# Moving operand tiles in SBUF: a two-layer diffusion-transformer kernel with new places for its weight, retention and column tiles

## The chip, the core and the metric

The kernel runs on one core of a Trainium2 chip. The metric is the device time of one execution in microseconds (us), lower is better. The core's engines are named as in the profile: PE (TensorE matmul) and PEld (its weight loads), DVE (VectorE), ACT (ScalarE), POOL (GpSimd) and SP, whose queue issues most DMAs.

## The reference

The model has two layers over 256 latent tokens `x` and 256 context tokens `ctx`, width 1024. Each layer modulates its input with a shift and a scale taken from a conditioning vector, mixes tokens, adds the gated result to the residual, normalizes, and does the same with an MLP.

```python
for i in range(2):
    mod = silu(c) @ ada_w[i] + ada_b[i]                 # shift, scale, gate, twice (and for ctx)
    h, hc = x * (1 + sc1) + sh1, ctx * (1 + sc1c) + sh1c
    y, yc = retention(h, hc) if i == 0 else neighbourhood_attention(h, hc)
    x = layer_norm(ALPHA * x + g1 * y)
    h = x * (1 + sc2) + sh2
    x = layer_norm(ALPHA * x + g2 * (square(relu(h @ mlp_w1[i])) @ mlp_w2[i]))   # 1024 -> 4096 -> 1024
    # in layer 0 ctx takes the same two steps; in layer 1 it ends here
```

Retention has 4 heads. A head projects to q and k (256 columns each), v and a gate g (512 each), forms masked scores over the 512 tokens, normalizes `scores @ v` per token, multiplies by `silu(g)` and multiplies the result (512 columns) by its rows of `ret_w_o`. All is float32.

## The kernel before

A matrix product in float32 is made of three products of a shorter float type (float32r): each operand is held as a high part and the low rest, and `mm3` issues high x high, high x low, low x high into one PSUM bank. `nc.tensor.matmul` takes a stationary operand (`lhsT`, 128 columns, loaded by an LDWEIGHTS on PEld) and a moving operand (`rhs`, 256 or 512 columns here). While PE streams the moving operand of one matmul, PEld loads the stationary operand of the next.

Weights come in units of 512 KB, `[128, k, ncol]` with 1024 numbers to a partition. `specs` lists all units in the order of their use. `fetch` loads the next one (`raw`, issued by SP), ACT casts it to the high part `hi`, and `lows` lets DVE subtract to get the low part `lo`. `hi` and `lo` come from two pools, `hip` and `lop`, of five buffers each (`WB`), 4096 bytes to a partition. `take` hands out units and fetches ahead. In the first phase, which goes by chunks of 128 rows, the class `Weights` uses the same two pools with 768 columns.

What is stationary and what moves:

- First MLP (layer 0), first product (`mm1`, and `ctx_mm1` for the context half of the first two): the weight unit is stationary, `hTh`/`hTl` (the modulated input, `[128, 8, 512]`) moves. Sixteen steps in all: two halves `hf` of eight `fp`, each with two units. Steps 0 and 1 of the first half go in 256-wide matmuls (latent half, then context half), the other fourteen in 512-wide ones, 48 matmuls a step.
- First MLP, second product (`mm2`): `hid`, the squared relu of the first product, is stationary, the unit moves. Two `hf`, two column halves, eight units `u`, 24 matmuls of 512 columns a unit.
- Retention: q and k with the unit stationary, v and gate with the unit moving. The head's output, transposed by `to_oT` into `oh` (high, ACT) and `ol` (low, DVE), is stationary for `tok_mm`, which has the `ret_w_o` units moving: bank `pw`, 96 matmuls a head, 384 in all.
- Layer 1: the neighbourhood attention (banks `pn`, `pnv`, `pqk`, `ppt`, `pav`, `pnw`), then an MLP whose first product has 256-wide matmuls. Its input is kept 448 bytes further on in `hTh`/`hTl` (`AT = 7 * LINE`, `LINE` being 16 numbers), and its opening (`p1t`) has these tiles stationary.

Tiles are laid out in SBUF in the order of their pools: small ones (`smp`), columns and constants (`cpool`: among them `cT`, `misc`, `lgn`, then `R`, `hTh`, `hTl`), `raw`, the weights, eight scratch tiles (`scp`), and nine slots of 8 KB (`arena`, taken by `slot`) that hold `hid`, `oh`, `ol` and others in turn. In the built program before, `hTh` starts at byte 40,608 of a partition, the first `hi` at 97,952, the first `lo` at 118,432 and slot 0 at 155,296: all of the large tiles are 32 bytes past a multiple of 64, and all stand alike within 512 bytes. So the stationary and the moving operand of nearly every 512-wide matmul start at the same place of a 512-byte stretch.

The order of instructions on ACT, DVE, POOL and PE is a scheduler's, except where `InOrder` pins it (`act.on`, `pe.on` and so on); SP keeps program order. Every instruction is recorded by a helper, so the profile gives line 84 for nearly all; tiles tell them apart.

Of the kernel before, what the change touches and what calls it, by code (L numbers as in the profile page):

```python
# [10 lines left out]
F32 = mybir.dt.float32  # L11
F32R = mybir.dt.float32r
# [5 lines left out]
P = 128  # L18
D = 1024
KC = D // P  # L20
NT = 512
# [3 lines left out]
DK = 256  # L25
DV = 512
# [10 lines left out]
LINE = 16  # L37
# [67 lines left out]
def kernel(  # L105
# [23 lines left out]
    pe, act, dve, pool, sp = (  # L129
        InOrder(tc, getattr(nc, e), e in PIN)  # L130
        for e in ("tensor", "scalar", "vector", "gpsimd", "sync")
    )
    ec = ctx.enter_context

    WB = 5
    smp = ec(tc.tile_pool(name="smp", bufs=4))
    cpool = ec(tc.tile_pool(name="cpool", bufs=1))
    rawp = ec(tc.tile_pool(name="rawp", bufs=4))
    hip = ec(tc.tile_pool(name="hip", bufs=WB))
    lop = ec(tc.tile_pool(name="lop", bufs=WB))  # L140
    scp = ec(tc.tile_pool(name="scp", bufs=8))
    arena = ec(tc.tile_pool(name="arena", bufs=1))
    dram = ec(tc.tile_pool(name="dram", bufs=1, space=DRAM))
    psp = ec(tc.tile_pool(name="psp", bufs=8, space=PSUM))

    def small(pool_, n, tag, **kw):

# [4 lines left out]
    def nm(s):  # L152
        uid[0] += 1
        return f"{s}_{uid[0]}"
# [4 lines left out]
    def slot(i, shape, dt, s):  # L159

        return arena.tile(shape, dt, tag=f"s{i}", name=nm(s))
# [4 lines left out]
    def tsl(t):  # L166
        return slice(t * P, (t + 1) * P)
# [6 lines left out]
    def mm3(o, a, b, start, stop):  # L174
        (ah, al), (bh, bl) = a, b
        pe.matmul(o, lhsT=ah, rhs=bh, start=start, stop=False)
        pe.matmul(o, lhsT=ah, rhs=bl, start=False, stop=False)
        pe.matmul(o, lhsT=al, rhs=bh, start=False, stop=stop)
# [4 lines left out]
    specs = []  # L183

    def w_rows(wt, r0, nr, c0, ncol):
        specs.append((wt[r0 : r0 + nr, c0 : c0 + ncol], nr // P, ncol))
# [17 lines left out]
    def spec_w1(l, f0):  # L204
        for u in range(2):
            w_rows(mlp_w1[l], 512 * u, 512, f0, 256)

    for hf in range(2):
        for fp in range(8):
            spec_w1(0, hf * 2048 + fp * 256)  # L210
        for half in range(2):
            for u in range(8):
                w_rows(mlp_w2[0], hf * 2048 + u * 256, 256, half * 512, 512)

    NW, NWO = nat_w_in[0], nat_w_o[0]
# [35 lines left out]
    units = []  # L251
# [3 lines left out]
    def fetch(n, in_scratch=False, at=None):  # L255

        for src, k, ncol in specs[len(units) : len(units) + max(n, 0)]:
            raw = rawp.tile([P, k, ncol], F32, tag="raw", name=nm("raw"))
            sp.dma_start(out=raw[:], in_=src.rearrange("(k p) n -> p k n", p=P))
            if in_scratch or len(units) in scratch_units:  # L260
                hi, lo = Rows([scr("hi", F32R) for _ in range(k)]), Rows([scr("lo", F32R) for _ in range(k)])
                for i in range(k):
                    act.copy(out=hi[:, i, :], in_=raw[:, i, :])
                    pending.append((lo[:, i, :], raw[:, i, :], hi[:, i, :]))
                units.append((hi, lo))
                continue
            if at is None:
                hi = hip.tile([P, k, ncol], F32R, tag="hi", name=nm("hi"))
                lo = lop.tile([P, k, ncol], F32R, tag="lo", name=nm("lo"))
            else:  # L270
                both = slot(at, [P, 2, k, ncol], F32R, "hilo")
                hi, lo = both[:, 0], both[:, 1]
            act.copy(out=hi[:], in_=raw[:])
            pending.append((lo[:], raw[:], hi[:]))
            units.append((hi, lo))
# [33 lines left out]
    ident = cv("ident")  # L309

    lnT = cpool.tile([P, 2, 2, 2, KC], F32, tag="lnT", name="lnT")
    cT = cpool.tile([P, KC, 16, 2], F32, tag="cT", name="cT")
    scol = cpool.tile([P, 2, KC], F32, tag="scol", name="scol")
    bcol = cpool.tile([P, 2, KC], F32, tag="bcol", name="bcol")
    acol = cpool.tile([P, 3, 2, KC], F32, tag="acol", name="acol")
# [43 lines left out]
    still = scr("still", F32R)  # L359
    dve.memset(still[:, :256].bitcast(F32), 1.0)  # L360

    misc = cpool.tile([P, 40], F32, tag="misc", name="misc")
    mhalf, onecol, lgm = misc[:, 0:1], misc[:, 1:34], misc[:, 36:40]
    dve.memset(mhalf[:], -0.5)

# [139 lines left out]
    def bg_stream():  # L505


        plan = []
        for l, w, part in (
            list(EARLY)  # L510
            + [(1, 0, 0), (1, 0, 1), (1, 0, 2), (1, 1, 0), (1, 1, 1), (1, 1, 2)]
        ):
            sh, sc, g = 3 * w * D, (3 * w + 1) * D, (3 * w + 2) * D
            offs = (sh + 512 * part, sc + 512 * part) if part < 2 else (g, g + 512)
            for n in range(KC):
                plan.append((l, w, part, offs, n))
        nxt = bg_load(*plan[0])
        yield
        for step, (l, w, part, offs, n) in enumerate(plan):
            raw = nxt  # L520
            if step + 1 < len(plan):
                nxt = bg_load(*plan[step + 1])

            nt = 2 if l == 0 or (w == 0 and part < 2) else 1
            if n == 0:
                red = smp.tile([P, 2, 32], F32, tag="red", name=nm("red"), bufs=2)
            if (l, w, part) in EARLY:
                dve.on = True
                for kk in range(2):
                    for t in range(nt):  # L530
                        weigh(spare(t), raw[:, kk, :], t, 2 * (n % 4) + kk, n % 4 == 0 and kk == 0)
                dve.on = False
                if n % 4 == 3:
                    yield
                    for t in range(nt):
                        folded(red, spare(t), t, 512 * (n // 4), 512)
            else:
                if n == 0:
                    acc = slot(S_VL, [P, 2, D], F32, "acc")
                for t in range(nt):  # L540

                    dve.on = n == 0 and (w, part) == (0, 0)
                    weigh(acc[:, t], raw[:].rearrange("p a n -> p (a n)"), t, n, n == 0)
                    dve.on = False
                if n == KC - 1:
                    for t in range(nt):
                        folded(red, acc[:, t], t, 0, D)
            if n == KC - 1:
                if part < 2:
                    due.append(lambda a=(l, w, red, 4 * part, nt): ada_columns(*a))  # L550
                else:
                    due.append(lambda a=(l, w, red, nt): ada_gate(*a))
            yield
# [162 lines left out]
    S_TH, S_TL, S_VH, S_VL, S_GS, S_SH, S_SL, S_T0, S_T1 = range(9)  # L716
# [20 lines left out]
    class Weights:  # L737
# [9 lines left out]

        def high(self, cols=slice(0, DK + DV)):
            if cols.start == 0:
                self.hi = hip.tile([P, DK + DV], F32R, tag="hi", name=nm("hi"))  # L750
            act.copy(out=self.hi[:, cols], in_=self.raw[:, cols])

        def low(self, cols=slice(0, DK + DV)):
            if cols.start == 0:
                self.lo = lop.tile([P, DK + DV], F32R, tag="lo", name=nm("lo"))
            dve.tensor_sub(out=self.lo[:, cols], in0=self.raw[:, cols], in1=self.hi[:, cols].bitcast(F32))

    def chunk_loads(k):
# [49 lines left out]
    prs, pts, rows = {}, {}, {}  # L808
# [15 lines left out]

    def chunk_row(k, cols=slice(0, 2 * P)):
        if cols.start == 0:
            rows[k] = smp.tile([P, 256], F32, tag="row", name=nm("row"), bufs=1)
        dve.tensor_copy(out=rows[k][:, cols], in_=prs[k][:, cols])

    def chunk_columns(k):  # L830
# [46 lines left out]
    def part_v(k, a, b):  # L877
# [8 lines left out]
        out=lgn[:, 0], in_=ret_decay[0].rearrange("(o d) h -> o (d h)", o=1).broadcast_to([P, 8])  # L886
# [19 lines left out]
    w = ws[0]  # L906
# [98 lines left out]
    for h in range(RH):  # L1005
# [9 lines left out]
        else:  # L1015
# [15 lines left out]
            for u in range(4):  # L1031
                ((wh, wl),) = take(1)
                for t in range(4):
                    for kk in range(2):
                        k = 2 * u + kk
# [72 lines left out]
        for t in range(4):  # L1108
            po = bank("po")
            scs = list(range(4)) if t < 2 else [2, 3]  # L1110
            for i, sc in enumerate(scs):
                a, b = S[sc]
# [12 lines left out]
            if t == 0:  # L1125
                bg()

        oh = slot(S_TH, [P, 4, NT], F32R, "oh")
        ol = slot(S_TL, [P, 4, NT], F32R, "ol")

        def to_oT(t):
            pT = bank("pT")
            for i in range(4):
                pe.transpose(pT[:, tsl(i)], gs[:, t, tsl(i)], ident)
            pv_ = pT[:].rearrange("p (k t) -> p k t", k=4)
            act.copy(out=oh[:, :, tsl(t)], in_=pv_)
            pinned, dve.on = dve.on, True
            dve.tensor_sub(out=ol[:, :, tsl(t)], in0=pv_, in1=oh[:, :, tsl(t)].bitcast(F32))
            dve.on = pinned

        between = {4: lambda: to_oT(0), 5: lambda: to_oT(1)}
# [7 lines left out]
        def tok_mm(t, half, us):  # L1149
            pw = bank("pw")  # L1150
            for k in range(4):
                wh, wl = us[k // 2]
                mm3(pw[:], (oh[:, k, tsl(t)], ol[:, k, tsl(t)]), (wh[:, k % 2, :], wl[:, k % 2, :]), k == 0, k == 3)
            return pw

        def tok(t, half, us):
# [120 lines left out]
    for hf in range(2):  # L1277
# [65 lines left out]
        for half in range(2):  # L1343
# [66 lines left out]
            p = turn(0)  # L1410
# [9 lines left out]
            p = turn(1)  # L1420
# [423 lines left out]
    n = NS - 1  # L1844
# [369 lines left out]
```

## Time and profile before

| | |
|---|---|
| time, median of 3 runs | 1178.7 us (1178.62 to 1179.35) |
| span of the profiled execution | 1177.4 us |
| PE busy | 1167.3 us, 6821 matmuls |
| PEld busy | 985.6 us, 6821 loads |
| DVE / ACT / POOL busy | 844.6 / 480.6 / 212.5 us |
| DMA | 195.10 MB, mean 166 GB/s |

The time holds 1.3 us beside the span of the profiled execution. [...] What a matmul costs in a stream is the distance between two starts: the chain of waits gives it as the length of a merged piece over its count. In rows of groups, `p<-hi,hid` means that bank `p` is written from tiles `hi` and `hid`.

### The profile page before, as it was taken

What the parts mean: (1) busy time and instruction counts of PE and PEld (TensorE: products, weight loads), DVE (VectorE), ACT (ScalarE), POOL (GpSimd) and SP (SyncE); (2) the same over time, 40 slices, a digit from 0 to 9 for tenths busy, and PEclk for the clock granted to TensorE, in tenths of its full rate; (3) what the DMA queues carried; (4) which work ended last, traced back from release to release, by engine and by line L of the source; (5) the groups of instructions that cost most, each with busy time, mean ns of one, the idle gap of its engine ahead of it and who ended that gap; (6) DMA issues with size and microseconds to landing.
All of it is one profiled execution on the core that took longest, in us unless ns stands there. A gap on an engine that the chain in (4) does not pass through costs nothing.

```text
span 1177.4 us, 17745 instructions
## 1 busy us (share of the span) xinstructions
PE 1167.3 (99%) x6821; PEld 985.6 (84%) x6821; DVE 844.6 (72%) x1349; ACT 480.6 (41%) x819; POOL 212.5 (18%) x364
## 2 busy tenths in 40 slices
PE   9999999999999999999999999999999999999997
PEld 7788888888888889888888888889888878999886
DVE  3786678787888787757767675678577589877446
ACT  3643332222323246442212333137466666665341
POOL 0103001000200241780203000223343430000001
PEclk9999999999999999999999999999999999999999
DMA  9943544544355416757566665646344334766660
GB/s 276 276 130 104 161 143 140 152 147 152 118 169 175 141 60 214 189 112 217 171 190 197 212 199 190 201 141 204 83 135 139 111 115 155 222 209 197 233 212 36
DMA packets 140115, 195.10 MB, mean 166 GB/s; under 512 B 9936, under 2 KB 81136, under 8 KB 140032
## 3 DMA queue, kind: packets, MB, share of 16 engines
q1 hardware_dynamic: 131904, 182.03, 49.4%
q0 software_dynamic: 6976, 9.39, 3.9%
q10 hardware_dynamic: 1152, 2.56, 0.7%
q8 instruction: 53, 0.87, 0.3%
q14 instruction: 30, 0.25, 0.1%
HBM read 189.12 MB, written 5.75 MB: 166 GB/s over the span
## 4 chain that ended last, share of the span: by engine, by line
PE 94%; DMA 2%; SPq 1%; ACT 1%; DVE 1%; issue 0%; POOL 0%; ACTq 0%; DVEq 0%
PE p L84 44%; PE pw L84 7%; PE pg L84 7%; PE pq L84 7%; PE pv L84 7%; PE pn L84 5%; PE pnv L84 4%; PE po L84 3%; PE ppt L84 2%; PE pnw L84 1%; PE pS L84 1%; PE pav L84 1%; PE pqk L84 1%; SPq L84 1%; PE pt L84 1%; PE p1t L84 1%
## 5 line engine op out<-in xcount | busy, mean ns | idle before, releaser
L84 ACT CAST hi<-raw 128x1024 fp32r<-128x1024 f32 (+2 forms) x228 | 231.7, 1032 | 308.9 <-PE p L84 113.4
L84 DVE TENSOR_TENSOR lo<-raw,hi 128x1024 fp32r<-128x1024 f32 (+2 forms) x228 | 273.4, 1213 | 105.5 <-ACT hi L84 105.4
L84 PE MATMUL p<-hi,hid 128*128 128x512 f32 (+1 forms) x832 | 241.8, 373 | 0.0
L84 PEld LDWEIGHTS p<-hi,hid 128*128 128x128 f32 x832 | 152.1, 188 | 27.6
L84 PE MATMUL p<-hTh,lo 128*128 128x256 f32 (+1 forms) x512 | 165.8, 326 | 0.0
L84 PE MATMUL p<-hTl,hi 128*128 128x256 f32 (+1 forms) x512 | 165.8, 326 | 0.0
L84 PE MATMUL p<-hTh,hi 128*128 128x256 f32 (+1 forms) x512 | 162.9, 328 | 0.0
L84 PE MATMUL p<-lo,hid 128*128 128x512 f32 (+1 forms) x416 | 155.2, 373 | 0.0
L84 DVE SCALAR_TENSOR_TENSOR acc<-rawa,scol,acc 128x1024 f32<-128x1024 f32 x56 | 74.5, 1342 | 66.0 <-DMA rawa<-in_ada_w_dram 66.0
L84 PEld LDWEIGHTS p<-hTh,lo 128*128 128x128 f32 x512 | 96.4, 188 | 8.8
L84 PEld LDWEIGHTS p<-hTl,hi 128*128 128x128 f32 x512 | 96.4, 188 | 8.7
L84 PEld LDWEIGHTS p<-hTh,hi 128*128 128x128 f32 x512 | 94.2, 188 | 8.7
L84 PEld LDWEIGHTS p<-lo,hid 128*128 128x128 f32 x416 | 78.4, 188 | 13.7
L84 DVE SCALAR_TENSOR_TENSOR strips<-rawa,scol,strips 128x512 f32<-128x512 f32 x112 | 78.6, 762 | 0.0
L84 ACT CAST hid<-r 128x256 fp32r<-128x256 f32 (+1 forms) x64 | 31.9, 500 | 111.2 <-DVE r L84 111.2
L84 POOL TENSOR_TENSOR rstd<-rstd,misc 128x1 f32<-128x1 f32 x28 | 19.1, 684 | 212.4 <-DVE rstd L84 211.4
L84 POOL TENSOR_TENSOR R<-R,acc 128x512 f32<-128x512 f32 x16 | 25.8, 1633 | 168.8 <-DVE acc L84 168.8
L84 ACT ACTIVATE s<-s,mn 128x512 f32<-128x512 f32 x64 | 45.5, 713 | 22.0 <-DVE mn L84 22.0
L84 PE MATMUL pw<-hi,oh 128*128 128x512 f32 x128 | 51.0, 398 | 0.0
L84 PE MATMUL pg<-hi,hTh 128*128 128x512 f32 x128 | 50.6, 395 | 0.0
L84 PE MATMUL pq<-hTh,hi 128*128 128x512 f32 x128 | 49.3, 395 | 0.8 <-ACT hTh L84 0.5
L84 PE MATMUL pw<-hi,ol 128*128 128x512 f32 x128 | 49.9, 390 | 0.0
(238 smaller groups left out, 2278.5 us busy)
## 6 DMA issues: line engine op xcount, KB each, us to landing
raw<-in_mlp_w_dram SPq DMA_DIRECT2D x128, 512.0 KB, 4.2
rawa<-in_ada_w_dram SPq DMA_DIRECT2D x80, 512.0 KB, 3.9
raw<-in_ret_w_in_dram SPq DMA_DIRECT2D x42, 512.0 KB, 3.9
raw<-in_nat_w_in_dram SPq DMA_DIRECT2D x24, 512.0 KB, 4.3
rawq<-in_ada_w_dram SPq DMA_DIRECT2D x16, 512.0 KB, 6.2
raw<-in_ret_w_o_dram SPq DMA_DIRECT2D x16, 512.0 KB, 3.4
bias<-rpb_rows POOLq DMA_DIRECT2D x32, 128.0 KB, 2.9
raw<-in_nat_w_o_dram SPq DMA_DIRECT2D x8, 512.0 KB, 3.8
```

The source lines that it names most:

```text
L84: r = f(*args, **kwargs)
```

## The change

- `hip` and `lop` become one pool `wpp`. Its tile holds both parts of a unit, 2 x 1024 numbers and 128 to spare. `wpair(at)` gives the high part at `at` and the low part 4096 bytes behind it. `Weights` takes its two parts from the same pool, both when the high part is made.
- `places` gives a start to the units of the first MLP: step `fp` of the first product `64 * fp` bytes into its tile, unit `u` of the second product `64 * u`. All others start at 0.
- `oh` and `ol` change from `[128, 4, 512]` to `[128, 2, 512, 2]`: two row blocks of the head's output are interleaved, so that a stationary operand is read with a step of 8 bytes.
- `misc` grows from 40 to 112 numbers, which moves all behind it; `cT` and the two `row` buffers go to arena slots, `red` shares the buffers of `rt`. With all this `hTh` starts at byte 38,336, the first `w` at 95,680 and slot 0 at 155,584: the large tiles are at multiples of 64 bytes.

```diff
-    hip = ec(tc.tile_pool(name="hip", bufs=WB))
-    lop = ec(tc.tile_pool(name="lop", bufs=WB))
+    wpp = ec(tc.tile_pool(name="wpp", bufs=WB))
...
+    WSLOT = 1024
+    WPAD = 128
+
+    def wpair(at):
+
+        both = wpp.tile([P, 2 * WSLOT + WPAD], F32R, tag="w", name=nm("w"))
+        return both[:, at : at + WSLOT], both[:, at + WSLOT : at + 2 * WSLOT]
...
+    places = {}
     for hf in range(2):
         for fp in range(8):
+            for u in range(2):
+                places[len(specs) + u] = LINE * fp
             spec_w1(0, hf * 2048 + fp * 256)
         for half in range(2):
             for u in range(8):
+                places[len(specs)] = LINE * u
                 w_rows(mlp_w2[0], hf * 2048 + u * 256, 256, half * 512, 512)
...
             if at is None:
-                hi = hip.tile([P, k, ncol], F32R, tag="hi", name=nm("hi"))
-                lo = lop.tile([P, k, ncol], F32R, tag="lo", name=nm("lo"))
+                hi, lo = (w.rearrange("p (k n) -> p k n", k=k) for w in wpair(places.get(len(units), 0)))
...
-    cT = cpool.tile([P, KC, 16, 2], F32, tag="cT", name="cT")
+    cT = arena.tile([P, KC, 16, 2], F32, tag="s1", name="cT")
+    row2 = arena.tile([P, 2, 256], F32, tag="s0", name="row2")
...
-    misc = cpool.tile([P, 40], F32, tag="misc", name="misc")
+    misc = cpool.tile([P, 40 + 72], F32, tag="misc", name="misc")
...
-                red = smp.tile([P, 2, 32], F32, tag="red", name=nm("red"), bufs=2)
+                red = smp.tile([P, 2, 32], F32, tag="rt", name=nm("red"), bufs=2)
...
             if cols.start == 0:
-                self.hi = hip.tile([P, DK + DV], F32R, tag="hi", name=nm("hi"))
+                self.hi, self.lo = (w[:, : DK + DV] for w in wpair(0))
...
-            rows[k] = smp.tile([P, 256], F32, tag="row", name=nm("row"), bufs=1)
+            rows[k] = row2[:, k % 2]
...
-        oh = slot(S_TH, [P, 4, NT], F32R, "oh")
-        ol = slot(S_TL, [P, 4, NT], F32R, "ol")
+        oh = slot(S_TH, [P, 2, NT, 2], F32R, "oh")
+        ol = slot(S_TL, [P, 2, NT, 2], F32R, "ol")
...
-            act.copy(out=oh[:, :, tsl(t)], in_=pv_)
+            oh_, ol_ = (o[:, :, tsl(t)].rearrange("p a t i -> p a i t") for o in (oh, ol))
+            act.copy(out=oh_, in_=pv_)
...
-                mm3(pw[:], (oh[:, k, tsl(t)], ol[:, k, tsl(t)]), (wh[:, k % 2, :], wl[:, k % 2, :]), k == 0, k == 3)
+                a, b = (o[:, k // 2, tsl(t), k % 2] for o in (oh, ol))
+                mm3(pw[:], (a, b), (wh[:, k % 2, :], wl[:, k % 2, :]), k == 0, k == 3)
```

PE's instructions, those of SP and those of POOL keep their order. The scheduler moves some on DVE and ACT, since both parts of a unit are now taken from their pool at the same point. Two places show the kind of move. On DVE, in retention head 1, between the rotation of the q projection's first half (`t_217`, later `t_185`) and its second (`t_218`, later `t_186`), `lo` and its `raw` being a weight unit for the same head. Before:

```order
L84 TENSOR_TENSOR qkl_1321<-t_217_1390,qkh_1320 128x256 [waits Activation_49]
L84 TENSOR_TENSOR lo_1419<-raw_1416,hi_1418 128x1024 [waits DMAHW3_49,PE_49,Activation_49]
L84 TENSOR_TENSOR t_218_1399<-pq_1323,cst_82 128x256 [waits Activation_49]
L84 TENSOR_TENSOR t_218_1399<-pq_1323,cst_82 64x256 x2
L84 TENSOR_TENSOR qkl_1321<-pq_1323,qkh_1320 128x256
L84 TENSOR_TENSOR t_218_1399<-t_218_1399 128x256 [waits DVE_49]
L84 TENSOR_TENSOR qkl_1321<-t_218_1399,qkh_1320 128x256 [waits Activation_49]
```

Now:

```order
L84 TENSOR_TENSOR qkl_1290<-t_185_1356,qkh_1289 128x256 [waits Activation_49]
L84 TENSOR_TENSOR t_186_1365<-pq_1292,cst_79 128x256 [waits Activation_49]
L84 TENSOR_TENSOR t_186_1365<-pq_1292,cst_79 64x256 x2
L84 TENSOR_TENSOR qkl_1290<-pq_1292,qkh_1289 128x256
L84 TENSOR_TENSOR t_186_1365<-t_186_1365 128x256 [waits DVE_49]
L84 TENSOR_TENSOR w_1384<-raw_1382,w_1384 128x1024 [waits DMAHW3_49,Activation_49]
L84 TENSOR_TENSOR qkl_1290<-t_186_1365,qkh_1289 128x256 [waits Activation_49]
```

The unit's subtraction stands four rows later, behind most of the second half's rotation, and has lost its wait for PE. On ACT, in the first half of the first MLP, around the casts of the two units of a step (`hi`, later `w`) and the relu of the step before (`r`). Before:

```order
L84 CAST hi_4453<-raw_4451 128x1024
L84 CAST hi_4459<-raw_4457 128x1024
L84 ACTIVATE r_4417<-p_684_4351 128x512
L84 CAST hid_4349<-r_4417 128x512
L84 ACTIVATE r_4511<-p_694_4449 128x512
```

Now:

```order
L84 CAST w_4364<-raw_4362 128x1024
L84 ACTIVATE r_4328<-p_599_4264 128x512
L84 CAST w_4369<-raw_4367 128x1024
L84 CAST hid_4262<-r_4328 128x512
L84 ACTIVATE r_4420<-p_607_4360 128x512
```

The relu of the second bank of a step now stands between the two casts.

More of the change, by code (lines that the diff above doesn't have):

```diff
@@ L749, in high @@
             if cols.start == 0:
-                self.hi = hip.tile([P, DK + DV], F32R, tag="hi", name=nm("hi"))
+                self.hi, self.lo = (w[:, : DK + DV] for w in wpair(0))
             act.copy(out=self.hi[:, cols], in_=self.raw[:, cols])
         def low(self, cols=slice(0, DK + DV)):
-            if cols.start == 0:
-                self.lo = lop.tile([P, DK + DV], F32R, tag="lo", name=nm("lo"))
             dve.tensor_sub(out=self.lo[:, cols], in0=self.raw[:, cols], in1=self.hi[:, cols].bitcast(F32))
@@ L1134, in to_oT @@
                 pe.transpose(pT[:, tsl(i)], gs[:, t, tsl(i)], ident)
-            pv_ = pT[:].rearrange("p (k t) -> p k t", k=4)
-            act.copy(out=oh[:, :, tsl(t)], in_=pv_)
+            pv_ = pT[:].rearrange("p (a i t) -> p a i t", a=2, i=2)
+            oh_, ol_ = (o[:, :, tsl(t)].rearrange("p a t i -> p a i t") for o in (oh, ol))
+            act.copy(out=oh_, in_=pv_)
             pinned, dve.on = dve.on, True
-            dve.tensor_sub(out=ol[:, :, tsl(t)], in0=pv_, in1=oh[:, :, tsl(t)].bitcast(F32))
+            dve.tensor_sub(out=ol_, in0=pv_, in1=oh_.bitcast(F32))
             dve.on = pinned
```

## The prediction

> **What bounds the kernel now.** I read the engines' busy times first, then PE's own waits, then the chain of waits in short windows.
>
> ```profile
> span 1177.4 us, 17745 instructions
> PE 1167.3 (99%) x6821; PEld 985.6 (84%) x6821; DVE 844.6 (72%) x1349; ACT 480.6 (41%) x819; POOL 212.5 (18%) x364
> ...
> PE 94%; DMA 2%; SPq 1%; ACT 1%; DVE 1%; issue 0%; POOL 0%; ACTq 0%; DVEq 0%
> ```
>
> ```profile
> PE pq L84 <- DVE still L84: 1.2, 1, 1.2
> PE pq L84 <- ACT hTh L84: 0.5, 1, 0.5
> PE pq L84 <- DVE hTh L84: 0.4, 1, 0.4
> ```
>
> PE is busy for 1167.3 of 1177.4 us, 94% of the chain that sets the end is PE, and its whole list of waits for other engines adds up to 2.1 us, all of it in bank `pq`. So nothing that ACT, DVE or the queues do sooner can pay. PE keeps its instructions and their order. What can move the time is what one matmul costs in a stream, so I worked that out from the chain of waits: start, length, bank, count. The length over the count is the distance between two starts.
>
> ```profile
> 464.98 105.17 PE p L84 x464
> 448.93 12.12 PE p L84 x101
> 803.97 12.15 PE pn L84 x100
> 1010.91 69.13 PE p L84 x610
> 996.06 8.03 PE p1t L84 x68
> ```
>
> 1. First MLP, 512 columns, both operands alike within 512 bytes: 105.17 / 464 = 226.66 ns.
> 2. First MLP, 256 columns, alike: 12.12 / 101 = 120.0 ns. `pn` in layer 1, 256 columns, alike: 121.5 ns with some interruptions in it.
> 3. Last MLP, 256 columns, where `AT` puts the moving operand 448 bytes on, so that the next stationary stands 64 bytes ahead of it within 512: 69.13 / 610 = 113.33 ns.
> 4. Its opening `p1t`, 256 columns, where the stationary tile is the one moved: it stands 64 bytes behind: 8.03 / 68 = 118.1 ns.
>
> Rows 1 and 2 differ by 106.66 ns for 256 columns. So 256 columns take 106.7 ns to stream, 512 take 213.3, and what is left is 13.3 ns at either width. It does not grow with the columns; it belongs to the handover from one matmul to the next. Row 3 has 6.7 ns of it, half as much, and row 4 11.4 ns. The three full values are 13.3, 6.7 and 113.3, all multiples of 6.67 ns: I call that a step. A 512-wide stream in this kernel pays two steps a matmul, and the only known way to pay one is another place of one operand against the other.
>
> [...]
>
> **The change part by part.**
>
> *Places in the first MLP.* First product: seven of eight steps get a place, 14 of 16 steps over both halves; one of them, step 1 of the first half, is 256 wide. 13 steps x 48 = 624 matmuls of 512 columns have the stationary 64 to 448 bytes ahead of the moving operand. Second product: 2 halves x 2 column halves x 7 units x 24 = 672, with the moving operand ahead. Together 1,296, some 190 for each of the seven distances. The 256-wide step has 96 matmuls at 64 bytes ahead, which is row 3: 96 x 6.67 = 0.6 us saved.
>
> For the 1,296 there is no row at 512 columns. Two of the seven distances have a 256-wide row: 64 ahead saves 120.0 - 113.3 = 6.7 ns, 64 behind saves 120.0 - 118.1 = 1.9 ns. Since what is left over is the same at both widths where both can be seen, I carry it over, and take the mean of the two for all seven: 4.3 ns x 1,296 = 5.6 us. The bounds on this side: 1.9 ns each is 2.5 us, 6.7 ns each is 8.6 us. On the far side a stream may fall out of step, as these rows of the timeline show (start, duration), after an interruption by other matmuls:
>
> ```profile
> 626.12 0.39 PE L84 MATMUL p<-hTl,hi 128*128 128x512 f32 x1
> 626.35 0.40 PE L84 MATMUL p<-hTh,lo 128*128 128x512 f32 x1
> 626.58 0.39 PE L84 MATMUL p<-hTh,hi 128*128 128x512 f32 x1
> 626.81 0.40 PE L84 MATMUL p<-hTl,hi 128*128 128x512 f32 x1
> 627.04 0.39 PE L84 MATMUL p<-hTh,lo 128*128 128x512 f32 x1
> ```
>
> They start 230 to 231 ns apart, some 4 ns over row 1, before the stream falls back to 226.7. Row 4 against row 3 is the same: 118.1 against 113.3. So the bound above zero is about 4.4 ns x 1,296 = 5.7 us lost.
>
> *Pairs in retention.* `tok_mm` has 384 matmuls of 512 columns whose stationary is now read with a step of 8 bytes; its start stays alike with the moving operand, or 4 bytes off. No row has a stationary with such a step.
>
> ```profile
> 214.96 16.12 PE pw L84 x71
> L84 ACT CAST oh<-pT x16: 580/587/592, 102.4 to 418.8; 128x512 fp32r<-128x512 f32 x16
> L84 DVE TENSOR_TENSOR ol<-pT,oh x16: 669/684/692, 105.3 to 419.7; 128x512 fp32r<-128x512 f32 x16
> L84 PE MATMUL pw<-hi,oh x128: 389/389/501, 106.8 to 436.4; 128*128 128x512 f32 x128
> ```
>
> Now it is 16.12 / 71 = 227.0 ns. The load passes the places of the moving operand at another pace, which may free a step (384 x 6.67 = 2.6 us) or cost the 4.4 ns of a stream out of step (1.7 us). I take half of the 4.3 ns above, as the start is unchanged: 0.8 us saved.
>
> The writers now write with a step of 8 bytes: 16 casts of 587 ns, 16 subtractions of 684 ns. Between no cost and twice as long, 16 x 1.27 = 20 us if nothing covered it. It is covered: the first subtraction starts at 105.3 and would end at 106.7 if doubled, while the first `pw` matmul starts at 106.8 and reads `oh` alone; later ones have a whole block of twelve `pw` matmuls (2.7 us) in between. I take zero.
>
> [...]
>
> *Multiples of 64 bytes.* Every 256- and 512-wide matmul reads rows that started 32 bytes past a multiple and no longer do. No row of before is aligned, so it has no price from one; bounds are zero and one step for each matmul (a rival, below). I take zero.
>
> *Shared tiles and moved subtractions.* A unit's parts come free together, so a cast waits also for the last reader of the low part, one or a few matmuls on (0.23 us each):
>
> ```profile
> ACT hi L84 <- PE p L84: 113.4, 49, 4.4
> DVE lo L84 <- ACT hi L84: 105.4, 87, 3.9
> ```
>
> ACT waits there already, 113.4 us in 49 times, and PE for none of these casts: there are five buffers, and a unit feeds 24 matmuls or 5.4 us. Behind a waiting cast on ACT stand a relu and the next cast; PE would see them first as a wait for `hi`, which it has nowhere. DVE is 72% busy. If this cover went, 0.2 us for each of some 100 units is 20 us; I see nothing that takes it away, so zero. `cT`, `row` and `red` are small and early: zero, with a few tenths either way.
>
> Sum: 5.6 + 0.6 + 0.8 = 7.0 us saved. The span becomes 1170.4; with the 1.3 us that the time holds beside it, 1171.7. The profiled execution stands at the median (1178.7), so nothing is added for that.
>
> **The rivals.**
>
> *A step falls everywhere, by alignment.* 256 columns are 1,024 bytes, and 106.7 ns are 16 steps: a step is as long as 64 bytes of the moving row. A row 32 bytes off touches one stretch of 64 more, at 512 columns as at 256, and that could be the step that row 3 still pays. Aligned, all would lose it: some 3,860 matmuls of 512 columns x 6.67 = 25.8 us gives 1153; the 256-wide ones too, some 890 at 120.0 by a step (5.9 us) and 671 of the last MLP by what the loads leave, as these 128-wide ones come no closer than 1.20 / 11 = 109 ns:
>
> ```profile
> 850.83 1.20 PE ppt L84 x11
> ```
>
> 671 x 4.3 = 2.9 us; in all 34.6 us, 1144. For it: both widths have the same remainder. Against it: the remainder may be the handover itself, and rows 2 and 3 are both 32 off.
>
> *Nothing but the 96.* A 512-wide matmul has 213 ns for a load that 256-wide ones fit into 113, so its two steps may not come from a meeting of the two reads at all. Then places do nothing: 1178.7 - 0.6 = 1178. For it: no 512-wide stream shows less than 226.66. Against it: all of them stand alike.
>
> *Slower: streams out of step.* Place: the first MLP from 462 to 792 us and the `pw` banks. The two steps of a 512-wide matmul stay, and a distance that is neither zero nor 64 ahead keeps streams from falling back into step, as 64 behind does in row 4. Price 4.4 ns each: (1,296 + 384) x 4.4 = 7.4 us, less 0.6: 1185.5. It decides from some 680 of the 1,680 on, since 680 x 4.4 - 600 ns is 2.4 us. For it: row 4 stays 4.8 ns above row 3 in the mean of its 68. Against it: even row 4 is below row 2.
>
> **How the numbers follow.** Forecast .46, 1171.7, its own range 1166.5 (all 1,296 and the 384 and the 96 a step lower, 11.8 us) to 1175.5 (all as row 4, 3.1 us). Alignment .18, 1144 to 1153, some of it with the places' gain on top. Nothing .14, 1178. Out of step .22, 1179 to 1185.5. About 0.2%, 2.4 us, is what a measurement of this kernel can tell from no change. Faster: all of alignment and nearly all of the forecast, .62. Same: the third case and what of the others ends there, .15. Slower: .23. The range of 8 in 10 leaves out the lower part of alignment and the last of the slow case: 1147 to 1184.
>
> **What would show it.** In the chain of waits of the changed kernel, the first MLP by its steps: 48 matmuls of 512 columns, 226.7 ns at step 0 and 220.0 at step 1 of the second half, 224 to 225 at step 7, between them in the others; in the second product, unit 1 like step 7 and unit 7 like step 1. `pw` near 225 in place of 227.0. `pq`, `pv`, `pg` unchanged at 226.7, and the last MLP at 113.3: if these fall to 220 and 109, alignment is right. Distances of 231 in the first MLP would show the slow rival, and a wait of PE for `w` that the cover has gone. The forecast is wrong if places other than 64 ahead save nothing.

## The result and the profile after

The changed kernel takes 1185.5 us (1185.41 to 1186.2), before 1178.7: a ratio of 1.0057, 95% interval 1.0037 to 1.0077. It is slower by 6.8 us, where 7.0 us faster was forecast. The range ended at 1184.

The head of the page of the changed kernel and PE's list of waits:

```profile
span 1183.5 us, 17741 instructions
PE 1173.8 (99%) x6821; PEld 988.9 (84%) x6821; DVE 845.0 (71%) x1349; ACT 483.2 (41%) x819; POOL 212.7 (18%) x364
...
PE 97%; DMA 1%; DVE 1%; ACT 1%; issue 0%; POOL 0%; ACTq 0%; DVEq 0%
```

```profile
PE pq L84 <- DVE still L84: 1.2, 1, 1.2
PE pq L84 <- DVE hTh L84: 0.4, 1, 0.4
PE pc L84 <- DMA brow<-in_ada_b_dram: 0.2, 1, 0.2
```

The span grew by 6.1 us and PE's busy time by 6.5, with the same 6,821 matmuls. Its waits are 1.8 us, none for `w`, `oh` or `ol`. So the loss is in what one matmul costs. The chain of waits of the changed kernel gives that for each step of the first MLP (start, length, bank, count). These are steps 0 to 7 of the first product's second half:

```profile
618.38 10.22 PE p L84 x45
630.37 9.80 PE p L84 x42
640.87 10.22 PE p L84 x44
651.79 10.31 PE p L84 x45
664.33 9.30 PE p L84 x41
674.31 10.50 PE p L84 x45
685.28 10.69 PE p L84 x46
698.43 8.70 PE p L84 x38
```

| next stationary ahead by, bytes | 0 | 64 | 128 | 192 | 256 | 320 | 384 | 448 |
|---|---|---|---|---|---|---|---|---|
| ns from start to start | 227.1 | 233.3 | 232.3 | 229.1 | 226.8 | 233.3 | 232.4 | 228.9 |

The table repeats every 256 bytes, and the first half's 512-wide steps, 128 to 448 ahead, give the same: 232.2, 228.9, 226.7, 233.3, 232.7 and 228.9 ns. 226.7 is the least, at 0 and 256; 64 ahead costs a whole step of 6.67 ns more. From the second product (unit 1, which is 64 behind or 448 ahead, and unit 7, 64 ahead), and from 256-wide streams 64 ahead (step 1 of the first half; the last MLP's first 48; the rest of it):

```profile
535.07 4.82 PE p L84 x21
568.09 5.14 PE p L84 x22
457.48 4.95 PE p L84 x42
1010.60 5.30 PE p L84 x45
1016.69 70.39 PE p L84 x621
```

The second product, where it is the weight that moves, follows the same table: 229.5 and 233.6. So in these rows it is the distance that counts, not which of the two operands was moved. The 256-wide streams give 117.9, 117.8 and 113.35 ns, all at the same distance. `pw`, whose stationary has the 8-byte step, and `pq`, which was not touched, with the load groups of `pw` in the changed kernel:

```profile
214.74 16.34 PE pw L84 x70
231.77 21.09 PE pq L84 x93
L84 PEld LDWEIGHTS pw<-w,oh 128*128 128x128 f32 x256 | 49.1, 196 | 8.9
```

`pw` went from 227.0 to 233.4 ns, and its loads take 196 ns, where those of `pq`, `pv`, `pg` and the MLPs have 188. `pq` stays at 226.8.

The sum from these rows, each against 226.7: 336 matmuls at 64 and 320 bytes x 6.6, 384 at 128 and 384 x 5.6, 384 at 192 and 448 x 2.3, 192 at 256 x 0.1: 2.2 + 2.2 + 0.9 + 0 = 5.3 us. `pw` adds 384 x 6.4 = 2.5, the 96 256-wide ones take away 96 x 2.1 = 0.2. That is 7.6 us, against 6.1 in the span and 6.8 in the time. The difference was not traced further; times of one kernel spread by more (the kernel before, 29 times on one chip: 1178.3 to 1182.0).

### The profile page after: what moved, and what is told of

It is laid out like the page before. It is cut to its first block, busy times and chain, and to the rows that moved or that the text cites. A ratio compares the mean times of both kernels' runs of the same rounds, so it can differ in the third digit from the quotient of the medians.

```text
span 1183.5 us, 17741 instructions
## 1 busy us (share of the span) xinstructions
PE 1173.8 (99%) x6821; PEld 988.9 (84%) x6821; DVE 845.0 (71%) x1349; ACT 483.2 (41%) x819; POOL 212.7 (18%) x364
## 4 chain that ended last, share of the span: by engine, by line
PE 97%; DMA 1%; DVE 1%; ACT 1%; issue 0%; POOL 0%; ACTq 0%; DVEq 0%
PE p L84 44%; PE pw L84 8%; PE pq L84 8%; PE pv L84 7%; PE pg L84 7%; PE pn L84 5%; PE pnv L84 4%; PE po L84 3%; PE ppt L84 2%; PE pnw L84 1%; PE pS L84 1%; PE pav L84 1%; PE pada L84 1%; PE pqk L84 1%; PE pt L84 1%; PE p1t L84 1%
## 5 line engine op out<-in xcount | busy, mean ns | idle before, releaser
L84 ACT CAST w<-raw 128x1024 fp32r<-128x1024 f32 (+2 forms) x224 | 231.0, 1038 | 324.1 <-PE p L84 164.9
L84 DVE TENSOR_TENSOR w<-raw,w 128x1024 fp32r<-128x1024 f32 (+2 forms) x224 | 272.2, 1223 | 111.4 <-ACT w L84 111.0
L84 PE MATMUL p<-w,hid 128*128 128x512 f32 (+1 forms) x1236 | 265.3, 375 | 0.0
L84 PEld LDWEIGHTS p<-w,hid 128*128 128x128 f32 x1236 | 218.8, 188 | 44.0
L84 PE MATMUL p<-hTh,w 128*128 128x256 f32 (+1 forms) x1024 | 240.8, 329 | 0.0
L84 PEld LDWEIGHTS p<-hTh,w 128*128 128x128 f32 x1024 | 171.9, 188 | 18.9
L84 PE MATMUL p<-hTl,w 128*128 128x256 f32 (+1 forms) x512 | 166.7, 328 | 0.0
L84 PEld LDWEIGHTS p<-hTl,w 128*128 128x128 f32 x512 | 96.3, 188 | 9.5
L84 PE MATMUL pw<-w,oh 128*128 128x512 f32 x256 | 81.7, 400 | 0.0
L84 PE MATMUL pq<-hTh,w 128*128 128x512 f32 x256 | 80.1, 392 | 0.4 <-DVE hTh L84 0.4
```

The lines of the kernel that those rows point to most:

```text
L84: r = f(*args, **kwargs)
```

## Experiments

All start from the changed kernel. The theory: what a 512-wide matmul costs follows the distance of stationary and moving operand, by the table above, and a stationary read with a step of 8 bytes costs about another step.

**No places.** All units back at the start of their tiles.

```diff
-                places[len(specs) + u] = LINE * fp
+                places[len(specs) + u] = 0
...
-                places[len(specs)] = LINE * u
+                places[len(specs)] = 0
```

> The changed kernel with every unit of the first MLP back at the start of its tile; pairs, shared tiles and multiples of 64 bytes stay. Theory (what a 512-wide matmul costs follows the distance between the next stationary and the moving operand): the first MLP's 512-wide matmuls all come back to 226.7 ns, which takes out (233.4-226.7) x 334 at 64 and 320 bytes, (232.5-226.7) x 383 at 128 and 384, (229.2-226.7) x 383 at 192 and 448: 2.2+2.2+1.0 = 5.4 us, and 96 256-wide ones go from 117.8 back to 120: 1180.3 us. Rival (shared tiles and moved subtractions cost the time): it stays at 1185.5.

Measured 1181.0 us, 1.0017 of before (1.0008 to 1.0026). In its chain, 203 matmuls of the second product, and `pw`:

```profile
580.99 46.01 PE p L84 x203
216.85 15.87 PE pw L84 x68
```

226.7 ns in the first MLP, 233.4 in `pw`. Against the changed kernel's 1185.5 the places cost 4.5 us of the 6.8; the shared tiles, which this run keeps, are not the cause of these.

**No pairs.** `oh` and `ol` as before, places kept.

```diff
-        oh = slot(S_TH, [P, 2, NT, 2], F32R, "oh")
+        oh = slot(S_TH, [P, 4, NT], F32R, "oh")
...
-                a, b = (o[:, k // 2, tsl(t), k % 2] for o in (oh, ol))
+                a, b = (o[:, k, tsl(t)] for o in (oh, ol))
```

> The changed kernel with oh and ol as before, so the stationary operand of the pw matmuls is read without a step; places stay. Theory: pw comes back from about 233.5 to 227 ns, 384 x 6.2 = 2.4 us: 1183.1 us, and the first MLP's table by distance stays as it is. Rival (shared tiles cost it): 1185.5. Rival (the writers' 8-byte step on ACT and DVE costs it): also about 1183, but with pw at 233 still.

Measured 1183.9 us, 1.0047 of before (1.0035 to 1.0059), and in the chain (`pw`, then step 1 of the second half):

```profile
217.95 12.24 PE pw L84 x54
628.37 10.04 PE p L84 x43
```

`pw` is back at 226.7 ns and step 1 stays at 233.5. Their share is 1.6 us; by the times alone that is not clear of the noise, since the changed kernel's interval is 1.0037 to 1.0077. This run takes away the writers' step as well as the readers', so it does not part the two by itself. The trace of the changed kernel does: PE waits there for neither `oh` nor `ol`, the cast into `oh` grew only from 587 to 626 ns and the subtraction from 684 to 685, while all 256 loads of `oh` take 192 to 201 ns, against 186 to 192 before. That holds for starts that are alike and for those 4 bytes off. So the pairs cost through PE's reading.

**Neither.** What is left of the change is the shared tiles, the moved casts and subtractions, and the multiples of 64 bytes.

> The changed kernel without places and without pairs: shared tiles and multiples of 64 bytes are left. Theory: 1185.5 - 5.2 - 2.4 = 1178 us, the same as before within 0.2%; the streams at 226.7, 120 and 113.3 ns as in the kernel before, so alignment to 64 bytes is worth nothing. Rival (shared tiles): slower than before by several us. Rival (alignment gains a step that places and pairs hid): 1150.

Measured 1178.9 us against 1179.0 for the kernel before on the same chip, 1.0001 (0.9992 to 1.001). These parts together cost and gain nothing that can be told. The last three runs were on one chip, so they can be compared without the changed kernel: 1183.9 with places alone and 1181.0 with pairs alone, against 1178.9, are 5.0 us for the places and 2.1 for the pairs. Alignment to 64 bytes is worth no step: 495 matmuls of the first MLP run at 112.21 / 495 = 226.7 ns, the last MLP's at 113.35.

```profile
461.94 112.21 PE p L84 x495
1003.77 5.06 PE p L84 x43
1009.98 70.05 PE p L84 x618
```

**One place of 256 bytes.** As the kernel with neither, with every unit of the first MLP 256 bytes into its tile.

```diff
-                places[len(specs) + u] = LINE * fp
+                places[len(specs) + u] = 4 * LINE
...
-                places[len(specs)] = LINE * u
+                places[len(specs)] = 4 * LINE
```

> As the kernel without places and pairs, but every unit of the first MLP starts 256 bytes into its tile, so every matmul of the first MLP has the operands 256 bytes apart. Theory (the price repeats every 256 bytes): 226.7 and 120 ns as with no distance, 1178 us. Rival (any distance other than zero lets streams fall out of step at their start): 1,440 x 4.4 ns = 6.3 us more, 1184.

Measured 1178.9 us, 1.0 of before (0.9991 to 1.0008). The second product, the last MLP's first 48, and the rest of it:

```profile
576.78 36.29 PE p L84 x160
1004.19 4.89 PE p L84 x43
1009.98 70.06 PE p L84 x618
```

36.29 / 160 = 226.8 ns: 256 bytes apart is as good as alike, so being apart does not by itself put a stream out of step. Beside it stands a finding on the 256-wide stream. The last MLP's first 48 matmuls cost 4.89 / 43 = 113.7 ns here and 5.06 / 43 = 117.7 in the run before it, and nothing differs at that place of the program, neither instructions nor addresses. At one distance a 256-wide stream has two rates. What decides between them, perhaps how the stream starts, was not tried by itself.

**One place of 64 bytes.** As the last, with `LINE` for `4 * LINE`.

> As the kernel without places and pairs, but every unit of the first MLP starts 64 bytes into its tile: one place, so no change from unit to unit. Theory (the distance sets the price): first product 672 x 6.6 ns, second product, 64 behind, 768 x 2.3 ns, 6.2 us more, less some 0.4 us of the 192 256-wide ones: 1184.7 us. Rival (the cost comes from changing the place between units, after which a stream must find its step again): 1179.

Measured 1185.5 us, 1.0048 of before (1.0035 to 1.0061). First product, then the second product's first column half, then a stretch of its second column half:

```profile
629.35 31.73 PE p L84 x136
527.82 44.80 PE p L84 x192
578.84 37.31 PE p L84 x163
```

31.73 / 136 = 233.3 ns without any change of place, so the cost does not come from the change from one unit to the next. But the distance alone does not set the price either. The second product is 64 behind throughout; it runs at 44.80 / 192 = 233.3 ns up to an interruption by eight `pada` matmuls at 578.2 us, and at 37.31 / 163 = 228.9 behind it. So a 512-wide stream, too, has two rates at one distance, and the table above gives those at which the changed kernel's streams ran. Some 216 matmuls at 4.4 ns more than the table are 1.0 us, and the run came out 0.8 us above the 1184.7 expected.

**Steps of 16 bytes.** As the kernel with neither, with places of 0 to 112 bytes.

```diff
-                places[len(specs) + u] = LINE * fp
+                places[len(specs) + u] = 4 * fp
...
-                places[len(specs)] = LINE * u
+                places[len(specs)] = 4 * u
```

> As the kernel without places and pairs, with steps of 16 bytes in place of 64 in the first MLP (0 to 112 bytes ahead in the first product, behind in the second). If the price goes by whole 64-byte pieces, distances under 64 cost 226.7 or jump once to 233.4; if it goes by the distance, it rises evenly from 226.7 at 0 to 233.4 at 64. A distance that gives 220 would be a way to gain; I expect none.

Measured once: 1185.4 us. Steps 1 to 7 of the second half, 16 to 112 bytes ahead, and unit 1 of the second product, 16 behind:

```profile
629.39 9.97 PE p L84 x44
639.82 10.73 PE p L84 x46
651.01 10.50 PE p L84 x45
662.83 10.26 PE p L84 x44
673.78 10.67 PE p L84 x46
684.90 11.01 PE p L84 x47
696.99 10.03 PE p L84 x43
579.18 4.62 PE p L84 x20
```

226.6 at 16 bytes, 233.3 at 32, 233.3 at 48, 233.2 at 64, 232.0 at 80, 234.3 at 96, 233.3 at 112. It jumps once, between 16 and 32, and does not rise evenly. 16 behind is 231.0, so the two sides are not alike here. No distance that was tried costs under 226.6, so none gave a 512-wide stream a step back.

**Eight places under 256-wide matmuls.** As the kernel with neither, with the places in the last MLP's first product.

```diff
     for fp in range(16):
+        for u in range(2):
+            places[len(specs) + u] = LINE * (fp % 8)
         spec_w1(1, fp * 256)
```

> As the kernel without places and pairs, with the units of the last MLP's first product at eight places 64 bytes apart: 256-wide matmuls at all eight distances. Prediction's assumption (what is left over a stream is the same at either width): 256-wide would cost 120 at 0 and 256 bytes, 126.7 at 64, which row 3 of the prediction contradicts. Theory now: the 256-wide table is its own, but repeats every 256 bytes too: 113.3 at 64 and 320, 120 at 0 and 256, 113 to 118 at 192 and 448; 128 is open.

Measured once: 1181.5 us, against 1179.05 for the kernel before, also once. In order of time 320, 384, 0, 64 and 128 bytes ahead:

```profile
1015.41 5.18 PE p L84 x44
1021.19 4.87 PE p L84 x41
1032.55 5.16 PE p L84 x43
1038.30 5.07 PE p L84 x43
1043.95 5.10 PE p L84 x43
```

117.7 at 320, 118.8 at 384, 120.0 at 0, 117.9 at 64, 118.6 at 128. 64 and 320 agree here too, and so do 128 and 384, but the order is turned round: 0 is the dearest for 256 columns and the cheapest for 512. The expected 113.3 at 64 did not come. The stream that before ran on for over 600 matmuls at 113.35 now changes its distance at each step and stands at 117.7 to 120.0: some 620 x 5 ns = 3.1 us, against 2.4 measured.

**Low part 64 bytes on; `hTl` 64 bytes on.** Two experiments on which pair of operands meets. As the kernel with neither, with only the low parts of the first MLP's units moved, and then with only the low part of the moving input moved.

```diff
-        return both[:, at : at + WSLOT], both[:, at + WSLOT : at + 2 * WSLOT]
+        return both[:, at : at + WSLOT], both[:, at + WSLOT + lo : at + lo + 2 * WSLOT]
...
-    hTl = cpool.tile([P, KC, NT], F32R, tag="hTl", name="hTl")
+    hTl = cpool.tile([P, KC * NT + 128], F32R, tag="hTl", name="hTl")
+    hTl = hTl[:, LINE : LINE + KC * NT].rearrange("p (k n) -> p k n", k=KC)
```

> As the kernel without places and pairs, but in the first MLP only the low part of a unit lies 64 bytes further on. In its first product the order is hTh with hi, hTl with hi, hTh with lo. If the price hangs on the stationary that is loaded while a matmul streams (the next one), the second of the three has its partner 64 bytes ahead and costs 233.4, the first and third 226.7. If it hangs on the matmul's own stationary, the third costs 233.4. By the mean both give 228.9 ns.

> As the kernel without places and pairs, but hTl (the low part of the moving input) stands 64 bytes further on than hTh. Of the first MLP's three matmuls (hTh with hi, hTl with hi, hTh with lo) the run with the low weights 64 bytes on had 228.4, 229.4 and 235.5 ns from their start to the next. If the price hangs on the matmul's own pair or on the stationary loaded meanwhile, the second of the three now is the dear one. If a start is late by what the matmul before it streamed against, the third is again the dear one. Either way the mean of three is some 228 to 231, not 226.7.

1186.6 and 1191.1 us, each measured once. With the low weights moved, the three matmuls of the first product have 228.4, 229.4 and 235.5 ns in the mean of some 220 each, 231.1 over all, which the chain shows too:

```profile
641.90 8.32 PE p L84 x36
```

The third is the dear one, whose own stationary is moved and whose successor's is not. With `hTl` moved all three stand at 231.4 to 232.6. The second experiment does not tell the cases apart, so it stays open whether a matmul's time hangs on its own stationary, on the one loaded meanwhile, or on what the matmul before it met. Both cost more than the table gives (228.9 was expected of the first), and the first of the three, whose own operands stand alike, rose as well, to 228.4: distances that differ from matmul to matmul disturbed the whole stream here. The 1191.1 us are not the first MLP's alone, since other products read `hTl` too.

**A place for 256-wide matmuls only.** As the kernel with neither, with 64 bytes for the units of steps 0 and 1, and of q and the first k of layer 1, which no 512-wide matmul uses.

```diff
-                places[len(specs) + u] = LINE * fp
+                places[len(specs) + u] = LINE * (hf == 0 and fp < 2)
...
+        if kind == "q" or (kind, i) == ("k", 0):
+            for u in range(2):
+                places[len(specs) + u] = LINE
```

> As the kernel without places and pairs, with a place of 64 bytes only for units that feed 256-wide matmuls alone: steps 0 and 1 of the first MLP and q and the first k of layer 1, 480 matmuls; no 512-wide stream is touched. Theory: they come from 120 to 117.8 ns when a stream does not fall into step and to 113.3 where it does: 1.1 to 3.2 us less than without, 1175.7 to 1177.9. Rival (256-wide gains only in the last MLP, by its own place of the input): 1178.9.

Measured 1177.7 us, 0.999 of before (0.998 to 0.9999). The first MLP's steps, and a stretch of `pn` against the same in the run with neither:

```profile
447.46 13.07 PE p L84 x111
805.24 10.38 PE pn L84 x89
```

```profile
802.50 14.18 PE pn L84 x117
```

13.07 / 111 = 117.7 ns, out of step; `pn` 116.6 with its interruptions, against 121.2. 1.2 us of a possible 3.2 came. It came out 0.1% below the kernel before, with an interval that ends at 0.9999, and it is the only use of places here that came out below it.

## Why the prediction was wrong

- **PE is the bound, and nothing else moves the time.** Right. PE's waits are 1.8 us, and the shared tiles and the moved subtractions cost nothing that can be measured: 1178.9 with these alone.
- **Handover.** This is the step that failed. From 13.3 ns left over at 512 and 256 columns alike I concluded that the rest belongs to the handover, is the same at either width, and that a gain seen at 256 columns holds at 512. The equality showed nothing: I had taken the time to stream 256 columns from the difference of the same two rows, so what was left had to come out equal. At 64 bytes ahead, by the same reckoning, a 512-wide matmul has 20.0 ns left over, a 256-wide one 6.7 to 11. The gain of one width is a loss at the other.
- **Places.** Forecast 5.6 us saved, from rows at 256 columns; the rows show 5.3 us lost, and the runs 4.5 and 5.0. The bound above zero, 5.7 us, held by luck: it stood on 4.4 ns for each matmul, and the rows show from 0.1 to 6.6 by distance, in long, even streams. The forecast's own range began at 1166.5; 1178.7 less the 11.8 of its terms is 1166.9, which changes nothing.
- **Row 3 as the price of a distance.** It is one of the two rates, 113.35 and 117.8 ns, at which 256-wide streams ran 64 bytes ahead. Row 4, read as the price of 64 behind, is of the same kind. The trace of before has a stretch of `p1t` at that distance which the prediction does not show:

```profile
991.17 0.62 PE L84 MATMUL p1t<-hi,hTh 128*128 128x256 f32 x4
991.62 0.62 PE L84 MATMUL p1t<-lo,hTh 128*128 128x256 f32 x4
992.07 1.07 PE L84 MATMUL p1t<-hi,hTh 128*128 128x256 f32 x8
```

Eight starts from 991.17 to 992.07 are some 113 ns each, not 118.1. So the two sides of the distance, which the forecast averaged to 4.3 ns, were two rates and not two prices. The 96 matmuls saved 2.1 ns each, not 6.67.

- **Pairs.** Forecast 0.8 us saved, between 2.6 saved and 1.7 lost; rows 2.5 lost, the runs 1.6 and 2.1. The 0.8 was half of the places' 4.3 ns and fell with it. PE waited for no writer, as forecast. But a stationary read with a step of 8 bytes was not free: the loads went from 188 to 196 ns and the matmuls from 227.0 to 233.4.
- **Alignment.** Taken as zero, and zero it is. That rival is gone: `pq` at 226.8, the last MLP at 113.35.
- **The slower rival** named the place and the size, 1185.5 us, and had .22. That the number came out to the tenth is luck: it took 4.4 ns for each of 1,680 matmuls, where the rows show 0.1 to 6.6, and 6.4 for `pw`. Its mechanism was half right. None is lost at 256 bytes (226.8 ns) and a full step at 64 ahead (233.3), so it is not any distance that costs; but that a stream can stay at a dearer rate until something interrupts it is what the 64-byte run shows, 233.3 and then 228.9 ns. I set it low because row 4 was below row 2, which is the same carrying over from 256 columns.

Places do count for 512-wide matmuls: the first product of the 64-byte run stands at 233.3 ns, beside 226.7 where the operands are alike. Whether it is the load of the next stationary that takes the time was not shown.

## What to carry to other kernels

When a kernel is PE's stream from end to end, divide a chain piece's length by its count and compare the streams; here a place in SBUF changed that by 3%, 226.7 to 233.3 ns. A price seen at one width of matmul was no price at another, as 64 bytes ahead took 512 columns up from 226.7 to 233.3 and 256 columns down from 120.0 to 117.8 or 113.35: find a row of the same width, or treat the sign as open. When a saving rests on a steady stream, look whether the same shape runs at two rates in the same trace, as 117.8 and 113.35, and 233.3 and 228.9, do here. And a remainder that is equal at two points shows nothing when the slope was taken from the same two points.

## What the runs showed of the hardware

- A 512-wide matmul in float32r cost 226.7 ns from start to start where the operands' starts were alike or 256 bytes apart. In the changed kernel it was 233.3 with the next stationary 64 and 320 ahead, 232.4 at 128 and 384, 229 at 192 and 448. At one distance, 64 behind, a stream ran at 233.3 over 192 matmuls and at 228.9 after an interruption (run with one place of 64 bytes).
- Whether the starts were 32 past a multiple of 64 did not matter: 226.66 ns before, 226.7 in the run with neither.
- A 256-wide one cost 120.0 ns at 0 and at 256 bytes (11.64 us for 97 in the run with one place of 256); at 64 it ran at 117.8 or at 113.35. What decides between the two rates of either width, and why the order of the distances differs between the widths, was not settled.
- A stationary read with a step of 8 bytes loaded in 196 ns in place of 188, and its stream ran at 233.4 ns in place of 227.0.
